# Moving the split weight tiles and the gated products of the MLPs by 64 bytes in SBUF

## The chip, the core and the metric

The kernel runs on one core of a Trainium2 chip. The metric is the device time of one execution in microseconds (us); smaller is better.

## The reference

A trunk of two layers over 512 tokens with 1024 channels, all in float32. Layer 0 is an mLSTM mixer, layer 1 a causal convolution module, and each is followed by the same kind of gated MLP. Ahead of every part stands an RMSNorm, behind it a residual sum.

```python
def conv_ffn(x, w_up, conv_w, conv_b, w_down):          # w_up 1024 x 5632, w_down 2816 x 1024
    hdn = causal_dwconv(x @ w_up, conv_w, conv_b)       # 3 taps
    return (jax.nn.silu(hdn[..., :D_FF]) * hdn[..., D_FF:]) @ w_down

for i in range(2):
    h = rmsnorm(x, norm_mix[i])
    x = x + (mlstm_mixer(h, ...) if i == 0 else conformer_conv_mixer(h, ...))
    x = x + conv_ffn(rmsnorm(x, norm_ffn[i]), f_w_up[i], f_conv_w[i], f_conv_b[i], f_w_down[i])
return rmsnorm(x, norm_final)
```

## The kernel before

Channels lie on the 128 partitions and the 512 tokens along the free axis. Each product of two float32 values is made of three float32r products: both sides are split into a high part (rounded to float32r) and a low part (the rest), and `mm3` (L160 to L163) issues high x high (L161), high weights x low input (L162) and low weights x high input (L163). Every matmul has its own weight load, which the engine can run beside the matmul ahead of it.

Weights come as units of 128 x 1024 floats in the order of their use. `feed_to` (L135) starts their transfers on the SP queue into `wr` (L140, four buffers), copies the high part on ScalarE (L149, tile `wh`) and subtracts on VectorE (L150, tile `wl`); `wh` and `wl` have three buffers each. `next_unit` (L154) hands a unit out with two more split ahead.

The stages in order of time, with what stands still in the array (the stationary side) and what streams through it (the moving side, named first in the profile's rows):

- `v_pair`: here the weights stream, and slices of the normed input `xh`, `xl` are stationary: 192 matmuls of 512 columns.
- `proj` (L404) for queries, keys and output gates, and, in layer 1, for the input of the convolution module (`glu`): weights stationary, `xh`, `xl` moving: 384 matmuls in each layer.
- attention: small products between tiles of the pool `mlstm`.
- `out_proj` (L560): weights stationary, the gated heads `gh`, `gl_` (layer 0) or the normed convolution `zht`, `zlt` (layer 1) moving: 192 matmuls each (L161 to L163, L576, L577, L580).
- `ffn` (L593), once per layer. Up: 22 pairs of `proj`, so 22 x 2 x 8 x 3 = 1056 matmuls with `xh`, `xl` moving. VectorE and ScalarE make the gated product from them and split it into `yh`, `yl` (L616, L617). Down: 8 output blocks of 22 x 3 = 66 matmuls with `yh`, `yl` moving: 528 in layer 0; in layer 1 the last block is done in two halves of 256 columns, which leaves 462 of 512 columns.

Where a tile lies follows from the pools, which are laid down one behind the other in the order in which they are opened: `const` (L49, with `xh`, `xl`), `wraw` (`wr`), `wsp` (`wh`, `wl`), `work` (sums and scratch tiles), and behind it whichever of `mlstm`, `ffn`, `conv` is open. Byte offsets within a partition, worked out from the sizes:

| tiles | offset of the first | modulo 128 | step from one to the next |
|---|---|---|---|
| `xh`, `xl` | 38464 | 64 | 2048 |
| `wr` | 71232 | 64 | 4096 |
| `wh`, `wl` | 87616 | 64 | 4096; a unit's k-th block of 128 columns lies 512 further each |
| `work` | 112192 | 64 (scratch tiles), 32 (`rsb`) | 2048 |
| `yh`, `yl` of both MLPs | 124672, 169728 | 0 | 2048 |
| `zht`, `zlt` | 175744, 194176 | 0 | 2048 |
| `gh`, `gl_` of heads 0 to 3 | 141568, 158080 | 0, 32, 64, 96 | 4128 |

The scores `sh` of the attention, the queries and keys `qkh`, `qkl`, and the selectors `sel` lie at 0 modulo 128, the constants `onesr`, `invdr` of the norms at 32.

Of the kernel before, what the change touches and what calls it, by code (L numbers as in the profile page):

```python
# [14 lines left out]
P = 128  # L15
# [9 lines left out]
EPS = 1e-6  # L25
QSCALE = 128.0 ** -0.5
NEG = -1.0e30
NPH = 4                    # token phases of the convolution on the tensor engine
NTAU = T // NPH
NJ = (CK + 2 * NPH - 3) // NPH  # L30
GR = 68                    # rows: input gates at 0, running maximum at 32, forget gates at 64

# column offsets in the packed per-channel parameter array
_COLS = {}
_off = 0
for _n, _w in [("norm_mix", 16), ("norm_ffn", 16), ("norm_final", 8), ("mconv_w", 32),
# [9 lines left out]
def hybrid_trunk(ctx, tc, x_in, par_in, tph_in, wg_in, wv_in, wqk_in, wo_in, mout_in, cin_in,  # L46
# [5 lines left out]
    wraw = ctx.enter_context(tc.tile_pool(name="wraw", bufs=4))  # L52
    wsp = ctx.enter_context(tc.tile_pool(name="wsp", bufs=3))
    work = ctx.enter_context(tc.tile_pool(name="work", bufs=1))
    psum = ctx.enter_context(tc.tile_pool(name="psum", bufs=6, space=bass.MemoryType.PSUM))
    psms = ctx.enter_context(tc.tile_pool(name="psms", bufs=2, space=bass.MemoryType.PSUM))

# [9 lines left out]
    def small():  # L67
        return psms.tile([P, T], F32, tag="ms", name=nm("ms"))

# [1 line left out]
    par = const.tile([P, NPAR], F32, name="par")  # L71
    nc.scalar.dma_start(out=par[:, :16], in_=par_in[:, :16])

# [18 lines left out]
    G.memset(mhalf, -0.5)  # L92

    def warm(n, after=None):
        """Products that nobody reads, to keep the clock of the tensor engine up over a wait."""
        ps = bank()
        for _ in range(n):
            with tc.issue_after(after.ins) if after is not None else nullcontext():
                after = PE.matmul(ps[:, :P], ones, ones, start=True, stop=True)  # L99

# [1 line left out]
    seq = []  # L102
    for h in range(2):
        for u in range(4):
# [57 lines left out]
        PE.matmul(ps, lh, rl, start=False, stop=False)  # L162
        PE.matmul(ps, ll, rh, start=False, stop=stop)  # L163

# [1 line left out]
    xh = [None] * KD  # L166
    xl = [None] * KD

# [27 lines left out]
        return t[:, c].rearrange("p (a b) -> p a b", b=P)  # L196

    def to_rows(src, c, tag):
        """Values along the free axis, equal on all partitions -> [128 tokens, blocks]."""
        nb = (c.stop - c.start) // P  # L200
        dg = work.tile([P, T], F32, tag="tmp", name=nm("dg"), bufs=4)
        V.tensor_tensor(out=blocks(dg, c), in0=src,
                        in1=ident[:].unsqueeze(1).to_broadcast([P, nb, P]), op=ALU.mult)
        r4 = work.tile([P, NTB], F32, tag=tag, name=nm(tag))
        V.tensor_reduce(out=r4[:, :nb], in_=blocks(dg, c), op=ALU.add, axis=mybir.AxisListType.X)
        return r4

    def from_rows(r4, nb, pb):
        """[128 tokens, blocks] -> the values along the free axis on all partitions (PSUM)."""
        hl = work.tile([P, 2, NTB], F32R, tag="hl", name=nm("hl"))  # L210
        V.tensor_copy(hl[:, 0, :nb], r4[:, :nb])
        V.tensor_tensor(out=hl[:, 1, :nb], in0=r4[:, :nb], in1=hl[:, 0, :nb], op=ALU.subtract)
        for i in range(2):
            dg = work.tile([P, NTB, P], F32R, tag="tmp", name=nm("dgr"), bufs=4)
            v = V.tensor_tensor(out=dg[:, :nb], in0=ident[:].unsqueeze(1).to_broadcast([P, nb, P]),
                            in1=hl[:, i, :nb].bitcast(F32).unsqueeze(2).to_broadcast([P, nb, P]),
                            op=ALU.mult)
            p = PE.matmul(pb, onesr, dg[:, :nb].rearrange("p a b -> p (a b)"), start=i == 0, stop=i == 1)  # L218
        return v, p

    def col_mean(ps, t, c, w):
        """Sum over the partitions of t times the constant in w, on all partitions."""
        h = work.tile([P, T], F32R, tag="tmp", name=nm("ch"), bufs=4)
        l = work.tile([P, T], F32R, tag="tmp", name=nm("cl"), bufs=4)
        A.copy(h[:, c], t[:, c])
        V.tensor_tensor(out=l[:, c], in0=t[:, c], in1=h[:, c], op=ALU.subtract)
        PE.matmul(ps, w, h[:, c], start=True, stop=False)
        PE.matmul(ps, w, l[:, c], start=False, stop=True)
# [4 lines left out]
        return o4  # L233

    def row_sums(ps, t, c, w, start, stop):
        """Adds the sums over the partitions of t, times w, to ps: [128 tokens, 2 * blocks]."""
        nb = (c.stop - c.start) // P
        for b in range(nb):
            s = slice(c.start + b * P, c.start + (b + 1) * P)
            PE.matmul(ps[:, 2 * b : 2 * b + 2], t[:, s], w[:, :2], start=start and b == 0,  # L240
                      stop=stop and b == nb - 1)

    def norm_rows(nrm, c):
        """1 / rms of the tokens in c, [128 tokens, blocks]."""
        n = c.stop - c.start
        ps = small()
        col_mean(ps[:, :n], nrm.acc, c, invdr)
        r4 = to_rows(ps[:, :n].rearrange("p (a b) -> p a b", b=P), c, "ms4")
        V.tensor_scalar(out=r4[:, : n // P], in0=r4[:, : n // P], scalar1=EPS, scalar2=None,
                        op0=ALU.add)  # L250
        return rsqrt4(r4, n // P, "rs4")

    # the row factors of a norm are worked out between the first products of the next stage
    hooks = []

    def run_hook():
# [15 lines left out]

    rs = {}

    # ================= layer 0: mLSTM =================
    warm(9)
    nrm = Norm()
    first = wraw.tile([P, 1024], F32, tag="wr", name="wr0")
# [76 lines left out]

    pv = v_pair(0)

    # gates, channel-major: input gates on partitions 0-3, forget gates on 32-35
    wgh, wgl = next_unit()
    pg = small()  # L360
    for k in range(KD):
# [77 lines left out]
    T0 = [0, 128, 256, 256]  # L439

    def att_decay(h):
        """exp of the decay from s to t less the running maximum; s on partitions, t free."""
        plf, pm = small(), small()
        for p, i in ((plf, h), (pm, NH + h)):
            PE.matmul(p, sel[:, i, :], sth, start=True, stop=False)
            PE.matmul(p, sel[:, i, :], stl, start=False, stop=True)
        es = []
        for i in range(NTB):
            t0 = T0[i]
            w = T - t0  # L450
            o = P + t0 - i * P
            e = mp.tile([P, T], F32, tag="se", name=nm("se"), bufs=4)
            V.tensor_tensor_scan(e[:, :w], plf[:, t0:], fm[:, o : o + w], NEG, ALU.add, ALU.max)  # L453
            es.append((i, t0, w, e))
        for i, t0, w, e in es:
            V.scalar_tensor_tensor(out=e[:, :w], in0=e[:, :w], scalar=li4[:, i, h : h + 1],
                                   in1=pm[:, t0:], op0=ALU.add, op1=ALU.subtract)
            A.activation(e[:, :w], e[:, :w], AF.Exp)
        return es
# [68 lines left out]
    q = qk(0)  # L528
# [60 lines left out]
    out_proj(gh, gl_, None, lambda m: ("norm_ffn", m))  # L589
    mctx.close()  # L590

    # ================= gated MLP with a depthwise convolution =================
    def ffn(l, g=None, last=False):  # L593
        fctx = ExitStack()
        fp = fctx.enter_context(tc.tile_pool(name=nm("ffn"), bufs=1))
        yh = fp.tile([P, NF, T], F32R, name=nm("yh"))
        yl = fp.tile([P, NF, T], F32R, name=nm("yl"))
        for j in range(NF):
# [91 lines left out]

    ffn(0, lambda m: ("norm_mix", 8 + m))

    # ================= layer 1: convolution module =================
    cctx = ExitStack()
    cp = cctx.enter_context(tc.tile_pool(name="conv", bufs=1))
    DVE_CH, POOL_CH, PE_CH = (0, 2, 4), (1,), (3, 5, 6, 7)
# [4 lines left out]
    pdvr = cp.tile([P, P], F32R, name="pdvr")  # L701
    A.copy(pdvr, p128)
    cacc = {c: cp.tile([P, T], F32, name=f"cacc{c}") for c in range(8)}
    # 1 where the partition lies in the block of NPH partitions
    tph = cp.tile([P, 8 * 4 * NJ * NPH], F32, name="tph")
    nc.sync.dma_start(out=tph, in_=tph_in)
    msk4 = cp.tile([P, P // NPH, 1], F32, name="msk4")
# [74 lines left out]
                o = 32 * (2 * hf + g)  # L782
                (nc.scalar if g == 0 else nc.sync).dma_start(out=back[o : o + 32], in_=co[:, g])

    # taps for the vector engine and GpSimd, handed out between the products
    vtaps, gtaps = [], []

    def background(nv, ng):
# [9 lines left out]
    FIRST, LAST = PE_CH[0], PE_CH[-1]  # L798

    def shift():  # L800
        """The mean of one block of channels, by which all values are shifted before their sums."""
        d[FIRST] = cp.tile([P, T], F32, name=f"d{FIRST}")
        A.activation(d[FIRST].rearrange("p (t q) -> p t q", q=NPH),
                     cacc[FIRST].rearrange("p (q t) -> p t q", q=NPH), AF.Identity,
# [56 lines left out]
    sq4 = stats(4, V)  # L861
    sq7 = stats(LAST, None)

    # layer norm over channels
    pr1, pr2, pmu = small(), small(), bank()
    for i, (t1, t2) in enumerate(((s1, s2), (d[LAST], sq7))):
        row_sums(pr1, t1, slice(0, T), invd, i == 0, i == 1)
# [34 lines left out]
def _layout(inputs):  # L902
    f = {k: np.asarray(v) for k, v in inputs.items()}

    def ch(a):  # [..., C] -> [128, ... * C/128], channel c = m * 128 + p
        a = a.reshape(a.shape[:-1] + (-1, P))
        return np.moveaxis(a, -1, 0).reshape(P, -1)

    def taps(w):  # [K, C] -> [128, C/128 * K]
        k, c = w.shape  # L910
        return w.reshape(k, c // P, P).transpose(2, 1, 0).reshape(P, -1)

    def cols(w, n=P):  # [K, N] -> [N/n, 128, K/128 * n]
        k, c = w.shape
        return w.reshape(k // P, P, c // n, n).transpose(2, 1, 0, 3).reshape(c // n, P, -1)

    # gate biases: input gates on partitions 0-3, forget gates on 32-35
    bg = np.zeros((P, 1), np.float32)
    bg[0:4, 0], bg[32:36, 0] = f["m_b_gates"][0][:4], f["m_b_gates"][0][4:]
    # taps by token phase: dph[c * NPH + p, m, g, j, q] = w[K - 1 - (NPH * j + q - p), m * 128 + g * 32 + c]  # L920
    dw = f["c_dw_w"][0].reshape(CK, KD, 4, P // 4)
    dph = np.zeros((P // NPH, NPH, KD, 4, NJ, NPH), np.float32)
    for p in range(NPH):
# [50 lines left out]
```

## Time and profile before

| | |
|---|---|
| median of 2 runs | 1194.37 us (1194.08 to 1194.66) |
| profiled execution, first to last instruction (span) | 1191.0 us |
| TensorE matmul busy | 1134.3 us (95%) |
| TensorE weight load busy | 939.7 us (79%) |
| VectorE busy | 788.6 us (66%) |
| ScalarE busy | 510.8 us (43%) |
| GpSimd busy | 174.8 us (15%) |

The page gives the span of the profiled execution and not its whole time; the median of the runs lies 3.4 us above that span. Matmuls overlap in the records: one begins before the end of the one ahead of it. So two numbers are read below: the distance from start to start of matmuls in a row (what a matmul costs), and the recorded length of one (the "mean ns"), which is some 162 ns longer than the distance and moves with it.

### The profile page before, as it was taken

Reading aid. Unit: us, or ns where it says so; the run is one execution under the profiler, and the core shown is the slowest. Engines: PE = TensorE matmul, PEld = TensorE weight load, DVE = VectorE, ACT = ScalarE, POOL = GpSimd, SP = SyncE. Lnnn points to the kernel's source line nnn. Section 1 sums busy time; section 2 is a strip of 40 time slices with the busy share of each in tenths; the row PEclk is TensorE's granted clock in tenths of the full one; section 3 lists DMA queues with packets and bytes.
Section 4 is the critical chain, followed back from the end, with each engine's and each line's share of the span. In section 5 each row is a group of like instructions: output and inputs, shape, how many; then the busy total and the mean of one; then the engine's idle time right before and its main releaser. Section 6 shows DMA issues by size and latency. Waiting matters only on the chain.

```text
span 1191.0 us, 13476 instructions
## 1 busy us (share of the span) xinstructions
PE 1134.3 (95%) x5226; PEld 939.7 (79%) x5226; DVE 788.6 (66%) x1022; ACT 510.8 (43%) x713; POOL 174.8 (15%) x126
## 2 busy tenths in 40 slices
PE   9999999999999999999998757699999999999996
PEld 7788888888888888888887647588888888888886
DVE  6788875487777775332479999874877777752222
ACT  6556774354444443222244522363544444432221
POOL 4000001100000000000267857021000000000002
PEclk9999999999999999999998879699999999999998
DMA  6222123223232323233332112022232323233322
GB/s 247 89 89 71 54 74 103 90 89 106 89 106 89 105 86 92 90 97 98 110 105 62 62 44 67 14 88 89 92 103 90 106 89 106 84 98 89 93 62 71
DMA packets 36369, 106.85 MB, mean 90 GB/s; under 512 B 4049, under 2 KB 10321, under 8 KB 36305
## 3 DMA queue, kind: packets, MB, share of 16 engines
q1 hardware_dynamic: 31728, 103.25, 27.2%
q10 hardware_dynamic: 4576, 2.74, 0.8%
q8 instruction: 41, 0.67, 0.2%
q14 instruction: 24, 0.19, 0.0%
HBM read 101.78 MB, written 2.10 MB: 87 GB/s over the span
## 4 chain that ended last, share of the span: by engine, by line
PE 84%; DVE 13%; issue 1%; ACT 1%; DMA 1%; POOL 0%; ACTq 0%; POOLq 0%; SPq 0%; DVEq 0%
PE mm L161 25%; PE mm L162 25%; PE mm L163 25%; DVE cacc L744 8%; PE mm L580 2%; PE mm L577 2%; PE mm L576 2%; DVE wl L150 2%; PE ms L240 1%; PE mm L99 0%; DMA xall<-in_dram 0%; PE ms L218 0%; DVE u L722 0%; DVE se L453 0%; DVE s L826 0%
## 5 line engine op out<-in xcount | busy, mean ns | idle before, releaser
L163 PE MATMUL mm<-xh,wl 128*128 128x512 f32 x960 | 375.6, 391 | 3.3 <-DVE wl L150 3.3
L161 PE MATMUL mm<-xh,wh 128*128 128x512 f32 x960 | 375.6, 392 | 0.0
L162 PE MATMUL mm<-xl,wh 128*128 128x512 f32 x960 | 375.4, 391 | 0.0
L150 DVE TENSOR_TENSOR wl<-wr,wh 128x1024 fp32r<-128x1024 f32 (+1 forms) x192 | 236.5, 1235 | 165.5 <-ACT wh L149 163.3
L149 ACT CAST wh<-wr 128x1024 fp32r<-128x1024 f32 (+1 forms) x192 | 197.4, 1030 | 296.1 <-PE mm L162 243.6
L163 PEld LDWEIGHTS mm<-xh,wl 128*128 128x128 f32 x960 | 181.4, 189 | 41.9 <-DVE wl L150 3.7
L162 PEld LDWEIGHTS mm<-xl,wh 128*128 128x128 f32 x960 | 181.4, 189 | 37.9
L161 PEld LDWEIGHTS mm<-xh,wh 128*128 128x128 f32 x960 | 181.5, 189 | 37.2
L193 POOL TENSOR_TENSOR acc<-acc,sq 128x512 f32<-128x512 f32 x30 | 43.3, 1444 | 746.7 <-ACT sq L191 746.2
L161 PE MATMUL mm<-yh,wh 128*128 128x512 f32 (+1 forms) x374 | 142.3, 380 | 0.0
L162 PE MATMUL mm<-yl,wh 128*128 128x512 f32 (+1 forms) x374 | 142.3, 380 | 0.0
L163 PE MATMUL mm<-yh,wl 128*128 128x512 f32 (+1 forms) x374 | 142.2, 380 | 0.0
L606 DVE TENSOR_TENSOR mm<-mm,rsb 128x512 f32<-128x512 f32 x88 | 60.8, 695 | 76.0 <-PE mm L163 73.1
L744 DVE SCALAR_TENSOR_TENSOR cacc<-u,par,cacc 128x501 f32<-128x501 f32 (+27 forms) x80 | 102.1, 1321 | 0.1
L161 PEld LDWEIGHTS mm<-yh,wh 128*128 128x128 f32 x374 | 70.0, 187 | 15.5
L162 PEld LDWEIGHTS mm<-yl,wh 128*128 128x128 f32 x374 | 70.0, 187 | 15.3
L163 PEld LDWEIGHTS mm<-yh,wl 128*128 128x128 f32 x374 | 70.0, 187 | 15.2
L616 ACT CAST yh<-ta 128x512 fp32r<-128x512 f32 x44 | 27.3, 620 | 104.6 <-DVE ta L615 104.6
L611 DVE SCALAR_TENSOR_TENSOR ta<-mm,par,ta 128x511 f32<-128x511 f32 x88 | 65.6, 745 | 1.3
L611 DVE SCALAR_TENSOR_TENSOR tb<-mm,par,tb 128x511 f32<-128x511 f32 x88 | 65.5, 746 | 1.4
L614 ACT ACTIVATE ta<-ta 128x512 f32<-128x512 f32 x44 | 27.8, 632 | 79.4 <-DVE ta L611 79.4
L741 POOL TENSOR_TENSOR cacc<-cacc,cprod 128x511 f32<-128x511 f32 (+29 forms) x30 | 49.5, 1651 | 24.1 <-ACT cprod L739 22.4
(237 smaller groups left out, 1200.5 us busy)
## 6 DMA issues: line engine op xcount, KB each, us to landing
wr<-in_dram SPq DMA_DIRECT2D x175, 512.0 KB, 3.5
wr<-in_dram SPq DMA_DIRECT2D x16, 384.0 KB, 3.1
xall<-in_dram SPq DMA_DIRECT2D x8, 256.0 KB, 6.4
us<-u ACTq DMA_DIRECT2D x16, 64.0 KB, 2.1
out_dram<-xall SPq DMA_DIRECT2D x2, 384.0 KB, 3.5
tph<-in_dram SPq DMA_DIRECT2D x1, 576.0 KB, 4.5
wr<-in_dram SPq DMA_DIRECT2D x2, 256.0 KB, 3.9
cacc<-co ACTq DMA_DIRECT2D x8, 64.0 KB, 2.4
```

The costliest lines, as they stand in the source:

```text
L149: st["last"] = A.copy(hi[:, :n], r[:, :n])
L150: V.tensor_tensor(out=lo[:, :n], in0=r[:, :n], in1=hi[:, :n], op=ALU.subtract)
L161: PE.matmul(ps, lh, rh, start=start, stop=False)
L162: PE.matmul(ps, lh, rl, start=False, stop=False)
L163: PE.matmul(ps, ll, rh, start=False, stop=stop)
L193: e.tensor_tensor(out=nrm.acc[:, c], in0=nrm.acc[:, c], in1=sq[:, c], op=ALU.add)
L606: V.tensor_tensor(out=ps, in0=ps, in1=rs["b"], op=ALU.mult)
L611: V.scalar_tensor_tensor(out=t[:, s:], in0=ps[:, : T - s], scalar=pcol("fconv_w", m * 3 + 2 - s), in1=t[:, s:], op0=ALU.mult, op1=ALU.add)
L614: A.activation(ta, ta, AF.Silu)
L616: A.copy(yh[:, j, :], ta)
L741: G.tensor_tensor(out=a[:, s:], in0=a[:, s:], in1=p[:, s:], op=ALU.add)
L744: V.scalar_tensor_tensor(out=cacc[j][:, s:], in0=u[:, : T - s], scalar=dw(j, CK - 1 - s), in1=cacc[j][:, s:], op0=ALU.mult, op1=ALU.add)
```

## The change

One tile of 64 bytes per partition that nothing uses is put at the head of the pool `wsp`, and one more at the head of the pool of the first MLP. No instruction is added or taken away. The rest of the diff takes out comments and docstrings, so the lines of the later code move up by a few.

```diff
     wsp = ctx.enter_context(tc.tile_pool(name="wsp", bufs=3))
     work = ctx.enter_context(tc.tile_pool(name="work", bufs=1))
+    wsp.tile([P, 16], F32, tag="pad", name="pad", bufs=1)
     psum = ctx.enter_context(tc.tile_pool(name="psum", bufs=6, space=bass.MemoryType.PSUM))
...
     def ffn(l, g=None, last=False):
         fctx = ExitStack()
         fp = fctx.enter_context(tc.tile_pool(name=nm("ffn"), bufs=1))
+        if l == 0:
+            fp.tile([P, 16], F32, name=nm("pad"))
         yh = fp.tile([P, NF, T], F32R, name=nm("yh"))
```

What moves, modulo 128: `wh`, `wl` from 64 to 0; everything behind them by 64 too, so `work` from 64 to 0, `zht`, `zlt` from 0 to 64, `gh`, `gl_` from 0, 32, 64, 96 to 64, 96, 0, 32, and `sh`, `qkh`, `qkl`, `sel` from 0 to 64; `yh`, `yl` of the second MLP from 0 to 64; those of the first MLP by 128, so they stay at 0. `xh`, `xl`, `wr` and the constants stay where they are.

## Rows read from the trace of the kernel before

**Rows 1.** The page, parts 1 and 4: span, busy times, chain by engine.

```profile
span 1191.0 us, 13476 instructions
PE 1134.3 (95%) x5226; PEld 939.7 (79%) x5226; DVE 788.6 (66%) x1022; ACT 510.8 (43%) x713; POOL 174.8 (15%) x126
...
PE 84%; DVE 13%; issue 1%; ACT 1%; DMA 1%; POOL 0%; ACTq 0%; POOLq 0%; SPq 0%; DVEq 0%
```

**Rows 2.** Busy time by stretch; columns as in the first line.

```profile
core 0: us, PE busy (x) PEld busy (x) DVE busy (x) ACT busy (x) POOL busy (x), PEclk, DMA share, GB/s
57.00:183.00 126.00, 125.07 (x637) 105.91 (x636) 103.09 (x193) 84.60 (x155) 4.04 (x4) 1.00 0.22 75
220.00:460.00 240.00, 240.00 (x1060) 198.67 (x1059) 175.63 (x226) 106.99 (x134) 1.02 (x1) 1.00 0.30 96
460.00:584.00 124.00, 124.00 (x534) 99.38 (x533) 39.90 (x43) 33.66 (x41) 7.77 (x6) 1.00 0.31 93
620.00:757.00 137.00, 93.33 (x521) 80.76 (x519) 136.90 (x122) 50.26 (x77) 92.62 (x54) 0.85 0.19 58
785.00:815.00 30.00, 30.00 (x133) 24.62 (x132) 19.64 (x21) 16.65 (x22) 9.25 (x6) 1.00 0.37 123
```

**Rows 3.** Groups by form, whole span: busy us, mean ns of one.

```profile
L161 PE MATMUL mm<-xh,wh 128*128 128x512 f32 x960 | 375.6, 392 | 0.0
L161 PE MATMUL mm<-yh,wh 128*128 128x512 f32 x330 | 130.0, 394 | 0.0
L162 PE MATMUL mm<-wl,xh 128*128 128x512 f32 x64 | 23.5, 389 | 0.0
```

**Rows 4.** Groups by form in 230 to 455 us, up of the first MLP.

```profile
L161 PE MATMUL mm<-xh,wh 128*128 128x512 f32 x330 | 128.4, 389 | 0.0
```

**Rows 5.** Groups by form in 462 to 582 us, down of the first MLP.

```profile
L161 PE MATMUL mm<-yh,wh 128*128 128x512 f32 x172 | 67.8, 394 | 0.0
```

**Rows 6.** Groups by form, output products of layer 1, then of layer 0.

```profile
L577 PE MATMUL mm<-zlt,wh 128*128 128x512 f32 x41 | 16.1, 392 | 0.0
...
L577 PE MATMUL mm<-gl,wh 128*128 128x512 f32 x46 | 18.1, 395 | 0.0
```

**Rows 7.** Timeline in the first up: start, length, instruction; two of 28.

```profile
399.78 0.39 PE L162 MATMUL mm<-xl,wh 128*128 128x512 f32 x1
...
405.90 0.39 PE L162 MATMUL mm<-xl,wh 128*128 128x512 f32 x1
```

**Rows 8.** Timeline in the first down: first and last of 27.

```profile
519.79 0.39 PE L162 MATMUL mm<-yl,wh 128*128 128x512 f32 x1
...
525.86 0.39 PE L161 MATMUL mm<-yh,wh 128*128 128x512 f32 x1
```

**Rows 9.** Timeline in the output product of layer 1: two, 13 steps apart.

```profile
787.84 0.39 PE L576 MATMUL mm<-zht,wh 128*128 128x512 f32 x1
...
790.81 0.39 PE L577 MATMUL mm<-zlt,wh 128*128 128x512 f32 x1
```

**Rows 10.** Groups by form in 93.70 to 93.72 us: the last matmul before attention.

```profile
L163 PE MATMUL mm<-xh,wl 128*128 128x512 f32 x1 | 0.4, 388 | 0.0
```

**Rows 11.** Groups by form in 592.56 to 592.59 us: the matmul before a norm's.

```profile
L162 PE MATMUL mm<-xl,wh 128*128 128x512 f32 x1 | 0.4, 396 | 0.0
```

**Rows 12.** Groups by form in 460.97 to 460.98 us: the first of down.

```profile
L161 PE MATMUL mm<-yh,wh 128*128 128x512 f32 x1 | 0.4, 394 | 0.0
```

**Rows 13.** Groups by form in 131.90 to 132.70 us: selectors, both sides at 0.

```profile
L445 PE MATMUL ms<-sth,sel 68*128 68x512 f32 x2 | 0.8, 396 | 0.0
```

**Rows 14.** Groups by form, VectorE, whole span: tiles at 0, then at 64.

```profile
L617 DVE TENSOR_TENSOR yl<-ta,yh 128x512 fp32r<-128x512 f32 x44 | 30.4, 691 | 26.1 <-ACT yh L616 26.1
...
L226 DVE TENSOR_TENSOR cl<-acc,ch 128x512 fp32r<-128x512 f32 x4 | 2.8, 689 | 2.1 <-ACT ch L225 2.1
```

**Rows 15.** Groups, GpSimd, whole span: sums at 0, then at 64.

```profile
L741 POOL TENSOR_TENSOR cacc<-cacc,cprod 128x511 f32<-128x511 f32 (+29 forms) x30 | 49.5, 1651 | 24.1 <-ACT cprod L739 22.4
L193 POOL TENSOR_TENSOR acc<-acc,sq 128x512 f32<-128x512 f32 x30 | 43.3, 1444 | 746.7 <-ACT sq L191 746.2
```

## The prediction

> **What bounds the kernel now.** The page comes first. TensorE is busy for 1134.3 of 1191.0 us and holds 84% of the chain that ended last; VectorE has 13% of it [rows 1]. The stretches then say where each of the two rules. In 220 to 460 us (up of the first MLP), 460 to 584 (its down) and 785 to 815 (output product of layer 1) TensorE is busy for the whole stretch, at a granted clock of 1.00, which is the level of 2.4 GHz. Only in 620 to 757 us, the convolution, is VectorE the full one (136.90 of 137.00 us), and TensorE has 93.33 us to do there [rows 2]. So almost everywhere the time is the number of matmuls times the distance from one to the next, and nothing else has to be late.
>
> Then that distance, stage by stage, because every stage streams the same 512 columns. At 2.4 GHz they would take 213.3 ns. In up, 27 steps take 405.90 - 399.78 = 6.12 us: 226.7 ns each [rows 7]. In down, 26 steps take 6.07 us, so about 233.4; the records come as 233, 233 and 234, and I use 233.3 [rows 8]. In the output product of layer 1, 13 steps take 2.97 us: 228.5 [rows 9]. The recorded length of one follows the distance and is read to the ns: 389, 394 and 392 [rows 4 to 6]; layer 0's output product has 395 [rows 6]. The number of matmuls, their clock and their weight loads are alike, so something else costs 6.6 ns per matmul in down. What differs is where the operands lie: up has the moving input at 64 and the weights at 64 modulo 128, down has the moving product at 0 and the weights at 64. The change moves just these.
>
> **The change part by part.** The two pads issue nothing: no instruction, no transfer, no wait, and no queue gets another order. Their cost can only come through addresses.
>
> *Copies, sums and transfers.* VectorE takes 691 ns for 512 elements with its tiles at 0 and 689 with them at 64 [rows 14]: I take 0. GpSimd's sums take 1651 ns at 0 and 1444 at 64 [rows 15], but the first run in the convolution beside a full VectorE and the second mostly do not, so the place need not be the cause. Were it, 30 taps would gain 0.2 us each, 6 us of GpSimd's time, and VectorE's bound would hide some of it: 0 to -6 us, taken as 0. Transfers land in `wr`, which stays.
>
> *Up: 2 x 1056 matmuls, weights from 64 to 0, input still at 64.* No long run of this pair exists before. Its nearest row is a matmul of `xh` beside which a weight block at 0 is loaded: it took 388 ns [rows 10], against 389 in the run of up [rows 4]. That is the last product of a `proj` before attention; there are eight such places (blocks of `sh`, `qkh` and `sel`), and all eight have 388. Where the next weights lie at 32 instead (the constants of a norm, twelve places with the same length), the same matmul takes 396 [rows 11], so one matmul does show a bad place at once; and the first matmul of down shows 394 [rows 12], the length of all that follow [rows 5]. Hence I take 0 for up. The bounds are -1 ns each (-2.1 us) and, if single cases mislead, the step of down, +6.6 ns each.
>
> Here the Trainium skill speaks against any effect (SBUF — State Buffer, section "Who interferes with whom"): the array reads its moving operand and its weights through two ports of their own. The two spacings of this trace, for equal work, do not agree with ports alone; by that rule the sum would be 0.
>
> *Second down: 462 matmuls, weights at 0, product from 0 to 64.* This is the pair of up after the change. If up keeps 226.7, down gets it too: 462 x 6.6 = -3.1 us. The bounds are that and 0.
>
> *First down: 528 matmuls, weights at 0, product at 0.* The nearest row has both at 0: the four selector products, 396 and 394 in mean [rows 13]. So 394 stays, and I take 0; the bounds are -3.5 us (528 x 6.6, if equal places are what counts) and +0.5 us (1 ns more).
>
> *Products of layer 0.* In `v_pair` the weights stream, so the moving side goes to 0 over stationary slices at 64, the pair of down before: 192 matmuls at 389 [rows 3] go to 394, +1.3 us. `proj` for queries, keys and gates is as up: 384 x 0. In attention and in the output product of layer 0 both sides move by 64 together: 0, with 192 x 6.6 = 1.3 us either way as the bound.
>
> *Layer 1.* The 384 matmuls of `glu` are as up, and where VectorE is full they lie beside it anyway. The output product's moving side goes from 0 to 64: 192 x (228.5 - 226.7) = -0.3 us.
>
> The sum: -3.1 - 0.3 + 1.3 = -2.1 us on a span of 1191.0, so 1188.9. The median of the runs lies 3.4 us above the span, so 1192.3.
>
> **The rivals.**
>
> *A, the sum above: the moving side's own place decides.* For it: rows 10 and 12. Against it: `zlt`, at 0 like `yh`, has 392 and not 394 [rows 5, 6], so modulo 128 is not the whole rule. About 1192; its own range is 1187 to 1195.
>
> *B, slower: what counts is whether the two sides lie alike.* Up is alike before (64 and 64) and fast, down is not (0 and 64) and slow. After the change up is unlike, by as much as down was. Then 2112 x 6.6 = +14.0 us, `proj` of layer 0 384 x 6.6 = +2.5, `v_pair` +1.3, `glu` some +1 (only its units ahead of 620 us), the first down becomes alike, -3.5, and the second stays unlike. Together +15.3: 1210. For it: the long runs are the bulk of the evidence and fit it. Against it: the eight matmuls of 388 with unlike sides, and selectors that are alike and slow [rows 10, 13]. It decides over A once up's distance grows by 2.1 / 2112 = 1.0 ns, to 227.7.
>
> *C, the place does nothing here.* The difference between up and down would come from something that they don't share, such as the second stream of VectorE and ScalarE beside up. All distances stay: 1194.4. The Trainium skill's rule of two ports, above, would have this one. Against it: twelve matmuls in the midst of a `proj`, with the same work around them, are 7 ns longer where the next weights lie at 32 [rows 11].
>
> *D, between A and B: up drifts.* The 388 of rows 10 is a little under up's steady 389, so a run of such matmuls may not hold its beat and, like the output product of layer 1, pay on some and not on others: 228.5 ns, 1.8 more. Then 2112 x 1.8 = +3.8, `proj` and `glu` +1, `v_pair` +1.3, second down 462 x (233.3 - 228.5) = -2.2: +3.9, 1198.
>
> *E, the floor falls.* No matmul of 512 columns is read below 388 in these rows, so 226.7 looks like the floor of this kernel. If weights at 0 took one more step of 6.6 ns away, up and `proj` would give 14.0 + 2.5 + 1 and the second down 3.1 and more: about 1173. The Trainium skill has 512 columns following each other by 512/2.4 + 2.5 ns, an estimate of 215.8 (TensorE: Matmul & The Clock Gate, section "Back-to-back issue gap"). No run of this trace comes near that.
>
> **How the numbers follow.** A 0.42, B 0.20, D 0.20, C 0.12, E 0.04, others 0.02. The time of the likeliest is 1192. A, C and D lie in 1187 to 1199 and hold 0.74, so the range must take in B, up to 1211; below 1187 lies E, which I leave out: 1187 to 1211. Faster or slower by over 2%, about what a measurement of this kernel can tell from no change, is under 1170.5 or over 1218.3. E reaches the first only with every bound at its end (0.02). B passes the second only if up's matmuls go to 396, or past it, and not to 394: 2112 x 8.3 = 17.5, with `proj`, `v_pair` and `glu` some 1217 to 1219 (0.03). All else, 0.95, is within 2%.
>
> **What would show it.** In the groups of the changed kernel: `xh` by `wh` in up at 388 or 389 (A, C, E lower) or at 394 (B) or between (D); `yh` by `wh` at 394 in the first MLP and 389 in the second (A), or 389 in the first and 394 in the second (B). `v_pair` at 394 speaks for A and B alike. The convolution's stretch should keep its 137 us of VectorE; if it shrinks, the GpSimd row was about the place after all. The prediction is wrong if up's length leaves 388 to 389: that one row carries 2112 matmuls, and each ns on it is 2.1 us.

## The result: 14 us longer, and the loss is in the up projections

The changed kernel takes 1208.17 us (2 runs, 1207.98 to 1208.37) against 1194.37 us before: the ratio is 1.012, 95% interval 1.0091 to 1.0149. That is less than 2%, but it is slower, where a gain of 2 us was forecast, and inside the range of 1187 to 1211, which reached that far because it took in rival B's 1210. The order of instructions on every engine is the one of before.

The page of the changed kernel answers to [rows 1]: span, busy time of each engine, shares of the chain that ended last.

```profile
span 1206.3 us, 13476 instructions
PE 1149.2 (95%) x5226; PEld 940.6 (78%) x5226; DVE 791.3 (66%) x1022; ACT 508.2 (42%) x713; POOL 174.6 (14%) x126
...
PE 84%; DVE 13%; issue 2%; ACT 1%; DMA 1%; POOL 0%; ACTq 0%; POOLq 0%; SPq 0%; DVEq 0%
```

The span grew by 15.3 us and TensorE's busy time by 14.9; every other engine moved by less than 3 us. That is 1.5 us more than the growth of the time, and the 3.4 us between span and time of the kernel before are no constant: in every other execution whose span is known the time lies 1.7 us above it, and a later execution of the kernel before with the same span of 1191.0 took 1192.74 us. So the profiled execution of the kernel before was a shorter one than the two that gave its time. The changed kernel's profiled execution has some 1.4 us at the start of layer 0 that this one lacks and that are no part of the change (last section); without them the span grew by 13.9. Where that lies is told by the groups by form (busy us, mean recorded length in ns). Of the changed kernel, in order: up of the first MLP (230 to 455 us), up of the second (850 to 1080), down of the first (480 to 590), down of the second (1100 to 1200), `v_pair` (12 to 50), output product of layer 1 (808 to 828), and of layer 0 (196 to 222). The lines of `mm3` are L162 to L164 here.

```profile
L162 PE MATMUL mm<-xh,wh 128*128 128x512 f32 x321 | 126.9, 395 | 0.0
...
L162 PE MATMUL mm<-xh,wh 128*128 128x512 f32 x316 | 125.0, 396 | 0.0
...
L162 PE MATMUL mm<-yh,wh 128*128 128x512 f32 x162 | 63.0, 389 | 0.0
...
L162 PE MATMUL mm<-yh,wh 128*128 128x512 f32 x113 | 44.7, 396 | 0.0
...
L163 PE MATMUL mm<-wl,xh 128*128 128x512 f32 x47 | 16.9, 391 | 0.0
...
L578 PE MATMUL mm<-zlt,wh 128*128 128x512 f32 x23 | 9.0, 391 | 0.0
...
L578 PE MATMUL mm<-gl,wh 128*128 128x512 f32 x39 | 15.4, 395 | 0.0
```

Up went from 389 [rows 4] to 395, the first down from 394 [rows 5] to 389; both output products stayed [rows 6]. The timeline in up (start, length, instruction) answers to [rows 7]:

```profile
398.67 0.40 PE L164 MATMUL mm<-xh,wl 128*128 128x512 f32 x1
398.90 0.39 PE L162 MATMUL mm<-xh,wh 128*128 128x512 f32 x1
399.13 0.40 PE L163 MATMUL mm<-xl,wh 128*128 128x512 f32 x1
...
401.00 0.40 PE L162 MATMUL mm<-xh,wh 128*128 128x512 f32 x1
```

Ten steps take 401.00 - 398.67 = 2.33 us: 233 ns from start to start, against 226.7 before. To the ns the steps alternate between 236 and 231, mean 233.3. The settled mean step is called the beat below. The recorded length is a rougher sign of it than [rows 4 to 6] suggested: a beat of 233.3 goes with 394 in down before, with 395 and 396 here, and with 397 and 398 in two runs below. Every time "from start to start" below is worked out in this way, over all the matmuls of its kind.

The stages, each from its first matmul to the first of the next, and the last one to the end of the span, in us (the output product of layer 0 took 45.1 in all of these and has no column; worked out from the same start times; the two kernels with half of the change and some others from below stand beside it):

| kernel | layer 0 to its output product | up 0 | down 0 | glu and convolution | output product 1 | up 1 | down 1 | span |
|---|---|---|---|---|---|---|---|---|
| before | 169.01 | 240.34 | 123.20 | 187.14 | 44.21 | 240.33 | 135.34 | 1191.0 |
| changed | 172.69 | 247.31 | 119.70 | 187.80 | 44.42 | 247.31 | 135.34 | 1206.3 |
| e_onlyw | 171.26 | 247.31 | 123.20 | 187.73 | 45.20 | 247.30 | 135.15 | 1208.6 |
| e_onlyp | 169.01 | 240.34 | 119.68 | 186.87 | 44.41 | 240.37 | 135.35 | 1187.5 |
| e_wsp256 | 170.57 | 240.34 | 123.20 | 186.83 | 44.43 | 240.34 | 135.34 | 1192.7 |
| e_y64 | 171.00 | 240.34 | 119.68 | 186.87 | 44.42 | 240.35 | 133.00 | 1187.2 |
| e_best | 169.02 | 240.34 | 119.68 | 186.63 | 44.09 | 240.32 | 132.82 | 1184.5 |

Both ups lose 7.0 us, the first down gains 3.5, the second stays: rival B, term by term.

### The profile page after: what moved, and what is told of

It is laid out like the page before. It is cut to its first block, busy times and chain, and to the rows that moved or that the text cites. A ratio compares the mean times of both kernels' runs of the same rounds, so it can differ in the third digit from the quotient of the medians.

```text
span 1206.3 us, 13476 instructions
## 1 busy us (share of the span) xinstructions
PE 1149.2 (95%) x5226; PEld 940.6 (78%) x5226; DVE 791.3 (66%) x1022; ACT 508.2 (42%) x713; POOL 174.6 (14%) x126
## 4 chain that ended last, share of the span: by engine, by line
PE 84%; DVE 13%; issue 2%; ACT 1%; DMA 1%; POOL 0%; ACTq 0%; POOLq 0%; SPq 0%; DVEq 0%
PE mm L162 25%; PE mm L163 25%; PE mm L164 25%; DVE cacc L747 8%; PE mm L581 2%; PE mm L578 2%; PE mm L577 2%; DVE wl L151 2%; PE ms L241 1%; DMA xall<-in_dram 0%; PE ms L219 0%; DVE u L725 0%; DVE se L454 0%; DVE s L829 0%; PE mm L518 0%
## 5 line engine op out<-in xcount | busy, mean ns | idle before, releaser
L164 PE MATMUL mm<-xh,wl 128*128 128x512 f32 x960 | 380.7, 397 | 3.5 <-DVE wl L151 3.5
L162 PE MATMUL mm<-xh,wh 128*128 128x512 f32 x960 | 381.0, 397 | 0.0
L163 PE MATMUL mm<-xl,wh 128*128 128x512 f32 x960 | 380.8, 397 | 0.0
L164 PEld LDWEIGHTS mm<-xh,wl 128*128 128x128 f32 x960 | 181.2, 189 | 47.8 <-DVE wl L151 3.9
L162 PEld LDWEIGHTS mm<-xh,wh 128*128 128x128 f32 x960 | 181.2, 189 | 43.2
L194 POOL TENSOR_TENSOR acc<-acc,sq 128x512 f32<-128x512 f32 x30 | 43.5, 1451 | 757.0 <-ACT sq L192 756.5
L162 PE MATMUL mm<-yh,wh 128*128 128x512 f32 (+1 forms) x374 | 141.7, 379 | 0.0
L164 PE MATMUL mm<-yh,wl 128*128 128x512 f32 (+1 forms) x374 | 141.6, 378 | 0.0
L162 PEld LDWEIGHTS mm<-yh,wh 128*128 128x128 f32 x374 | 70.3, 188 | 14.0
L163 PEld LDWEIGHTS mm<-yl,wh 128*128 128x128 f32 x374 | 70.3, 188 | 13.9
L164 PEld LDWEIGHTS mm<-yh,wl 128*128 128x128 f32 x374 | 70.3, 188 | 13.8
L744 POOL TENSOR_TENSOR cacc<-cacc,cprod 128x511 f32<-128x511 f32 (+29 forms) x30 | 49.1, 1635 | 25.4 <-ACT cprod L742 23.7
```

The costliest lines, as they stand in the source:

```text
L162: PE.matmul(ps, lh, rh, start=start, stop=False)
L194: e.tensor_tensor(out=nrm.acc[:, c], in0=nrm.acc[:, c], in1=sq[:, c], op=ALU.add)
L744: G.tensor_tensor(out=a[:, s:], in0=a[:, s:], in1=p[:, s:], op=ALU.add)
```

## The experiments

Four readings were open. **Distance** (rival B in a sharper form): what counts is how far the moving operand lies from the weights, modulo some length. **Own place**: the place of one side alone decides (the forecast, A). **Modulo 128**: as the distance, but 64 and 192 are the same thing, and 128 is no distance. **No place at all** (C). Offsets from here on are in bytes modulo 256, and a distance is the moving operand's offset less the stationary one's. By it, before: up 0 (64 and 64), down 192 (0 and 64), output product of layer 1 64 (128 and 64). After: up 192 (64 and 128), first down 0 (128 and 128), second down 192 (64 and 128), output product of layer 1 64 (192 and 128).

### Everything moved together (e_all64), and the gated products alone (e_y64)

`e_all64` puts a pad ahead of `xh` and all that follows it in memory:

```diff
+    const.tile([P, 16], F32, name="pad")
     mhalf = const.tile([P, 4], F32, name="mhalf")
```

`e_y64` puts one ahead of the gated products, in both MLPs:

```diff
+        fp.tile([P, 16], F32, tag="pad", name=nm("pad"), bufs=1)
         yh = fp.tile([P, NF, T], F32R, name=nm("yh"))
```

> The kernel before with everything from the normed input on moved by 64, so that both sides of every product move together: input and weights at 0, products of the MLPs at 64 modulo 128. Theories R and P: every distance stays, so 1194.4 us, up at 389 ns of length and down at 394. Rival M, by which weights at 0 are what made the changed kernel slow: up at 396 and some 1208 us.

> The kernel before with the gated products of both MLPs moved from 0 to 64 modulo 128 and the weights left at 64. Theory R: the distance of product and weights becomes 256, so both downs go from 233.3 to 226.7 ns: 990 x 6.6 = 6.5 us less, 1187.8 us, ratio 0.9945. Rival P: the same. Rival C (the place counts for nothing in down): 1194.4.

`e_all64` has the weights at 128, as the changed kernel has them, and the normed input moved along to 128. It took 1193.5 us, ratio 1.0008 [0.9998, 1.0018]. Its groups in up and in the first down, by form:

```profile
L162 PE MATMUL mm<-xh,wh 128*128 128x512 f32 x331 | 128.8, 389 | 0.0
...
L162 PE MATMUL mm<-yh,wh 128*128 128x512 f32 x165 | 65.0, 394 | 0.0
```

So the loss of the change is gone although the weights keep the address that they have in the changed kernel: their own place costs nothing. `e_y64` leaves the weights at 64 and puts the gated products there too (distance 0). It took 1187.8 us, ratio 0.9954 [0.9939, 0.9969]. That it met the forecast to the tenth is luck: the forecast started from 1194.4 us, and against 1192.8 for the kernel before in the same session the gain is 5.0 us and not 6.5. Down fell from 394 to 389 in both MLPs:

```profile
L161 PE MATMUL mm<-yh,wh 128*128 128x512 f32 x162 | 63.0, 389 | 0.0
```

The stages show 3.5 us of gain in the first down, as due for 528 x 6.6, but 2.3 in the second, where 462 x 6.6 = 3.0 were due. The rest went back in its last block, whose 132 products have 256 columns. The groups by form there, of before (1163 to 1190 us) and of `e_best` (1155 to 1183 us; below, the same places as `e_y64` in the MLPs):

```profile
L162 PE MATMUL mm<-yl,wh 128*128 128x256 f32 x44 | 12.3, 279 | 0.0
...
L162 PE MATMUL mm<-yl,wh 128*128 128x256 f32 x44 | 12.5, 285 | 0.0
```

From start to start these have a median of 113 to 114 ns before (distance 192) and of 120 in both later kernels (distance 0): at this width distance 0 is the slower one, and 132 products lose 0.8 us.

### The two halves of the change (e_onlyw, e_onlyp)

`e_onlyw` has the weight pad alone:

```diff
+    wsp.tile([P, 16], F32, tag="pad", name="pad", bufs=1)
```

`e_onlyp` has the MLP pad alone:

```diff
+        if l == 0:
+            fp.tile([P, 16], F32, name=nm("pad"))
```

> The weight half of the change alone: 64 bytes ahead of the split weight tiles, so that the weights lie at 128 modulo 256, and the gated products, which follow in memory, at 64 in both MLPs (in the changed kernel they were at 128 in the first). Distance theory (a beat is set by the moving operand's place less the weights', modulo 256; 0 gives 226.7 ns, 192 gives 233.3): up projections 233.3 as in the changed kernel, and both down projections at distance 192, so the first down projection loses what it had gained there: 384 products by 6.6 ns = 2.5 us above the changed kernel, so about 1210.7 us. Rival, the weights' own place alone sets the beat: the down projection of the first MLP stays at 226.7 ns as in the changed kernel, 1208.2 us.

> The other half alone: 64 bytes ahead of the gated products of the first MLP, nothing else. Weights at 64, gated products of the first MLP at 64, of the second at 0 as before. Distance theory: only the first down projection changes, 233.3 to 226.7 ns, 384 products by 6.6 = 2.5 us less than the kernel before, ratio 0.998. Rival, the weights' own place alone sets the beat: ratio 1.000, the first down projection stays at 233.3. Together with the other half the two should add up to the whole change: about +16.3 and -2.5 us.

`e_onlyw` took 1210.07 us, ratio 1.014 [1.0123, 1.0156]; `e_onlyp` 1189.04, ratio 0.9962 [0.9947, 0.9977]. The 2.5 us in both expectations was worked out with 384 products; the first down has 528, so 3.5 us were due, which is what the stages show (123.20 and 119.68). The two add up: +17.1 and -3.9 us against +13.8 for the whole change. The first down is slow again where only the weights moved (485 to 590 us, against 389 in the changed kernel), so the weights' own place is refuted here as well:

```profile
L162 PE MATMUL mm<-yh,wh 128*128 128x512 f32 x151 | 59.7, 396 | 0.0
```

One row of `e_onlyw` had not been expected, its output product of layer 1 (808 to 828 us):

```profile
L578 PE MATMUL mm<-zlt,wh 128*128 128x512 f32 x24 | 9.5, 398 | 0.0
```

Its operands lie at the very bytes where the changed kernel has them, and yet it runs at 398 and 233.3 ns from start to start, where the changed kernel has 391 and 228.9. At distance 64 the addresses alone don't fix the beat.

### The low weights 64 bytes off the high ones (e_wl64)

```diff
+    wsp.tile([P, 16], F32, tag="pad", name="pad", bufs=1)
     lo = wsp.tile([P, 1024], F32R, tag="wl", name="wl0")
```

> The kernel before with 64 bytes between the high and the low parts of the weights: wh at 64, wl at 0, and the products of the MLPs at 64. In up and down the distance is 0 for wh and 192 for wl. Theory R with the weights that are loaded beside a product: the product ahead of each one with wl (xl by wh) is long, the other two are not, some 228.9 ns on average, 1194.4 + 2112 x 2.2 - 990 x 4.4 = 1194.7 us. If the weights that stand in the array count, the product with wl is the long one, with the same average. If one long product shifts the phase for the others, all three forms change.

Here `wh` lies at 64 and `wl` at 128, so in up only one product in three, the one with `wl`, is off distance 0; it is at 192. It took 1205.1 us, ratio 1.0098 [1.0083, 1.0113]. In up, by form:

```profile
L163 PE MATMUL mm<-xh,wl 128*128 128x512 f32 x324 | 128.8, 397 | 0.0
L162 PE MATMUL mm<-xl,wh 128*128 128x512 f32 x324 | 127.0, 392 | 0.0
L161 PE MATMUL mm<-xh,wh 128*128 128x512 f32 x324 | 126.1, 389 | 0.0
```

From start to start these are 235.8, 229.2 and 228.4 ns: the product that uses the odd block is the long one, and the two behind it, which are at distance 0, don't come back to 226.7 before the next odd one. The mean, 231.1, is 4.4 above the floor, though two products of three are at distance 0: one odd block in three spoils the beat of all. The expectation had two of its readings come true together (the weights in the array count, and one long product shifts the others); its mean of 228.9 ns and its 1194.7 us were missed.

### The distance by itself (e_probe, e_probe2)

```diff
+            for b in list(range(0, 512, 16)) + [4, 8]:
+                run([b], [0])
+            for b in range(64, 512, 64):
+                run([0], [b])
+            run([0], [0, 0, 64, 64], 24)
+            run([0], [0, 0, 0, 0, 64, 64, 64, 64], 24)
```

> The kernel before with 786 more products ahead of the second MLP's down, which nobody reads; they cost what they take, so its time is not compared. 512 columns of yh move over blocks of yl; the distance of the moving side from the weights (modulo 512) is raised in steps of 16 bytes by moving the first (18 products each), then in steps of 64 by moving the second, then two mixed orders. Theory R (only the distance of the two sides modulo 256 counts): 226.7 ns from start to start at distance 0 and 256, 228.9 at 64 and 320, 233.3 at 192 and 448, and the same figures whichever side is moved; at 128 and 384 some value between 226 and 234. Rival P (only like or unlike modulo 128 counts): 226.7 at 0, 128, 256, 384 and one and the same slow value at 64, 192, 320, 448. Rival M (a side's own place counts): moving the weights by 64 does not give what moving the products by 448 gives. In the mixed orders a weight block at another distance should lengthen the product beside which it is loaded, or the one after it.

> Extra products, which nobody reads, ahead of the second down projection: runs of 18 at one distance, each of the first thirteen behind 18 products at distance 0, with the weights at 0, 64, 128 and 192. Question: in the first probe distance 64 took 233.3 ns behind a run at distance 48 and 228.9 ns behind a run at 0 (there the weights, not the moving operand, were shifted). If the history decides: distance 64 behind a run at 0 takes 228.9 ns whatever the weights' place, and 233.3 where a run at 32, 48 or 192 stands ahead of it. If the place decides: 233.3 with the moving operand at 64 and the weights at 0, 228.9 with the weights at 192, whatever stands ahead. Distance 192: 233.3 with every place if the distance alone decides. Steps of 4 bytes up to 256: the floor of 226.7 ns is a single place or a plateau from 240 on. With 384, 256 and 128 columns in place of 512: if the loss sits in the change from one product to the next it stays about 6.6 ns for a product of any length; if it goes with the words read, it shrinks to 3.3 ns at 256 columns.

The cut is from `e_probe`: a run is 18 products of `yh` blocks over `yl` blocks, with the moving side moved by `b` bytes in the first loop and the stationary side in the second. The products stand ahead of the second down and nobody reads them; each of the two kernels was executed once. From start to start, settled, 512 columns, ns (the steps of a run cycle through up to seven lengths, so the means are good to some 0.3):

```
distance      0    16    32    48    64    80    96   112   128   144   160   176   192   208   224   240   256
e_probe    226.7 231.5 233.5 233.3 233.3 231.0 233.1 231.0 232.5 233.3 234.0 233.4 233.3 234.6 233.3 226.7 226.7
e_probe2   226.7 231.8 233.2 230.0 228.9 231.5    -     -  233.2    -     -     -  233.3    -     -  236.7 226.7
```

From 272 to 496 `e_probe` repeats the values of 16 to 240 within 0.2 ns: the period is 256. Moving the stationary side instead gave 228.9 at distance 64, 233.3 at 192 and 226.7 at 256. A row by form for each of two settled runs: distance 0 in `e_probe2` (1253 to 1256 us, entered at 256) and 64 in `e_probe` (1073.3 to 1076.2 us):

```profile
L627 PE MATMUL mm<-yh,yl 128*128 128x512 f32 x15 | 3.6, 389 | 0.0
...
L627 PE MATMUL mm<-yh,yl 128*128 128x512 f32 x14 | 3.4, 397 | 0.0
```

"Modulo 128" and "no place" fall: 64, 128 and 192 all cost. In `e_probe2` distances 64 and 192 were run with the stationary side at 0, 64, 128 and 192, and 128 with it at 0, 64 and 128: the means did not differ by over 1 ns with the place. But 64, 48 and 240 have two beats each. Distance 64 came as 228.5 to 229.2 all eleven times in `e_probe2`, behind runs at 0, 32, 48, 80, 128 and 192, and as 233.3 behind 48 in `e_probe`. So neither theory in that expectation holds: the run before, as I had it, does not decide, and the place does not. Distance 240, at the same offsets, was 226.7 in `e_probe` (388) and 236.7 in `e_probe2`, here at 1119.3 to 1122.3 us and at 1236.5 to 1239.3 us:

```profile
L627 PE MATMUL mm<-yh,yl 128*128 128x512 f32 x15 | 3.6, 388 | 0.0
...
L627 PE MATMUL mm<-yh,yl 128*128 128x512 f32 x14 | 3.5, 400 | 0.0
```

Between 240 and 256 there is no plateau: 238.6 at 244, 233.3 at 248, 230.0 at 252. Only distance 0 was at 226.7 every time that it had settled. What picks one of two beats stays open. The run ahead and the place together are not ruled out: distance 64 with the moving side at 64 and the weights at 0 did not stand behind 48 again in `e_probe2`, and 240 stood behind 224 in `e_probe` and behind 232 in `e_probe2`.

The mixed runs show how a beat is entered and left. With four blocks at distance 0 and four whose weights lie 64 further (distance 192), in turns, the steps were (ns, from the start times; a bar where the blocks change):

```
228 233 230 226 | 236 231 236 229 | 231 231 235 232 | 226 236 231 235 | 229 232 231 226 | 236 231 235
```

In the first and the third turn the last product at distance 0 keeps its 226, though the load beside it is already that of the odd block, and the product that uses this block takes 236; in the second turn, entered before the beat had settled, the 236 comes one product later. The way back is slow: four products at distance 0 take 231, 231, 235, 232 in one turn and 229, 232, 231, 226 in the other. Runs of 18 at distance 0 settled at once or after up to ten steps (in `e_probe2` once 230, 236, 228, 233, 231, then 226.7).

Shorter products do not follow the same table (`e_probe2`, settled, one run each below 512, ns):

```
columns   distance 0     64    128    192
512            226.7  229.0  233.2  233.3
384            173.3  173.3  176.0  174.6
256            120.0  117.7  118.7  113.3
128            111.8  111.6  112.0  111.5
```

The loss is neither a fixed sum for each product nor in proportion to its words: at 256 columns distance 192 is the fastest and 0 the slowest, 6.7 ns apart, as in the last block of the second down, and at 128 no difference over 0.5 ns is left. The rows by form at 256 columns, for distance 0 (1270 to 1271 us) and 192 (1276 to 1277.3 us):

```profile
L627 PE MATMUL mm<-yh,yl 128*128 128x256 f32 x11 | 1.5, 283 | 0.0
...
L627 PE MATMUL mm<-yh,yl 128*128 128x256 f32 x14 | 1.8, 277 | 0.0
```

### The period in the whole kernel (e_wsp128, e_wsp256)

The pad of `e_wsp128`; in `e_wsp256` it has 64 columns in place of 32:

```diff
+    wsp.tile([P, 32], F32, tag="pad", name="pad", bufs=1)
```

> 128 bytes ahead of the split weight tiles: weights at 192 modulo 256, norm outputs left at 64, so the up projections are at distance 128; gated products at 128 (distance 192, as before), the conv module's output at 0 (distance 64, as before). Distance theory with period 256 and the probe's 232 to 232.5 ns at 128: 2112 up products by 5.3 to 5.8 ns = 11 to 12 us more, and some 2 us from the projections of layer 0: 1206 to 1208 us. Rival, only the place modulo 128 counts: 1194 us, up stays at 226.7 ns. The output products of layer 1 move their operand at 0 here and at 128 before, both 64 above the weights: the same 228.9 ns if the distance alone decides, 233.3 if the moving operand's own place takes part (the probe had 233.3 at distance 64 with the moving operand at 64).

> 256 bytes ahead of the split weight tiles: every distance is the same modulo 256 as in the kernel before, every one but that of products with all operands behind the pad is off by 256 modulo 512. Distance theory with period 256: no change, ratio 1.000, up projections 226.7 ns, down projections 233.3 ns. Rival, period 512 or more (the probe went only to 496 bytes with one pair of tiles): up projections 233 ns, some +14 us.

`e_wsp128` took 1212.27 us, ratio 1.0153 [1.0138, 1.0168]; `e_wsp256` 1192.69, ratio 1.0 [0.999, 1.0009]. Up in the one and in the other:

```profile
L162 PE MATMUL mm<-xh,wh 128*128 128x512 f32 x321 | 126.8, 395 | 0.0
...
L162 PE MATMUL mm<-xh,wh 128*128 128x512 f32 x330 | 128.4, 389 | 0.0
```

A step of 128 is as bad as one of 64, a step of 256 costs nothing: the period is 256 and not 128. `e_wsp128` came out 4 to 6 us above its 1206 to 1208. Up at distance 128 takes 233.3 ns in mean here and not 232 to 232.5 (247.26 us for a stage, close to the changed kernel's), which is some 2 us of that. Layer 0 to its output product took 173.64 us, 4.6 more than before where some 2 were expected; 2.0 of these 4.6 are the long first products of the last section. And its second down, at distance 192 as before, shows that the distance does not fix the beat at 256 columns either: the last block has a median step of 118 ns where the kernel before has 113, and is 0.5 us longer. Its output product of layer 1 (moving at 0, weights at 192) kept 229 ns.

### All products of 512 columns of the two MLPs and of layer 1's output at distance 0 (e_best)

```diff
+        fp.tile([P, 16], F32, tag="pad", name=nm("pad"), bufs=1)
         yh = fp.tile([P, NF, T], F32R, name=nm("yh"))
...
+    cp.tile([P, 48], F32, name="pad")
     cacc2 = cp.tile([P, T], F32, name="caccp")
```

> The gated products of both MLPs and the conv module's output put at 64 modulo 256, where the weights lie: 64 bytes ahead of the gated products, 192 bytes at the head of the conv module's pool. Distance theory: up and down projections 226.7 ns, output products of layer 1 from 228.9 to 226.7 (192 by 2.2 ns = 0.4 us below the kernel that aligned the gated products alone): ratio 0.9952 against 0.9955 there. Rival, the gain of that kernel was not the distance of the gated products: output products stay at 228.9 and the ratio is that of the other kernel.

1186.68 us, ratio 0.9951 [0.9937, 0.9964]: below both kernels. The output product of layer 1 has the floor now (785 to 808 us), 226.7 ns from start to start:

```profile
L577 PE MATMUL mm<-zlt,wh 128*128 128x512 f32 x36 | 14.0, 389 | 0.0
```

Its stage is 0.32 us shorter than in `e_y64`, where 0.4 was forecast. Against `e_y64` as a whole the two intervals overlap, so that step alone is not shown by the times.

## Why the prediction was wrong

**What held.** TensorE bounds the kernel and the time is the count of matmuls times their distance from start to start: the changed kernel's 15.3 us are TensorE's 14.9 us of busy time and little else. That the operands' places set the beat of up held too (up is alike in everything but address in `e_all64` and the changed kernel); elsewhere the places alone do not fix it (228.9 or 233.3 at distance 64). Copies and sums at nothing held: GpSimd's two kinds of sums have changed places and kept their lengths (1635 and 1451 ns, against 1651 and 1444 [rows 15]), so their difference is not the place, and VectorE still fills 137.43 of the 140 us of the convolution's stretch (630 to 770 us).

**The step that failed: "Hence I take 0 for up."** It was read from the eight matmuls of 388 ns beside which a weight block at 0 is loaded [rows 10], backed by one that showed 396 at another place [rows 11]. Up went to 395 and lost 2 x 7.0 us; with it the second down, which was to gain 3.1 as the pair of up, gained nothing. The mixed run shows why [rows 10] misled: on the way from distance 0 to 192 the product *beside* the first odd load keeps its 226 ns, and the product that *uses* that block pays. The 388 belonged to a product whose own weights were still at distance 0; behind it came products of attention, with another moving tile. Nor were all such places at 388. Three more matmuls of `xh` in the trace of before stand ahead of a block at 0 modulo 128 and are long, at 57.37, 58.14 and 174.68 us (400, 397 and 398 ns; ahead of `st`, of a selector, as three of the eight, and of `hn`); the first and the last of them:

```profile
L163 PE MATMUL mm<-xh,wl 128*128 128x512 f32 x1 | 0.4, 400 | 0.0
...
L163 PE MATMUL mm<-xh,wl 128*128 128x512 f32 x1 | 0.4, 398 | 0.0
```

[rows 11] taught the wrong lesson (one matmul shows a bad place at once), since a single transition can go either way: in `e_probe2` the last product of a run at distance 0, with its moving side at 0, took 232 to 233 beside the load of a block at 128, and 226 to 227 beside blocks at 0, 64 and 192. The first matmul of down with its 394 [rows 12] was read as support for A; it fits B as well.

**The other terms.** With the distance rule in A's place the working of B gives the stages: up +14.0 (measured 6.97 + 6.98), first down -3.5 (measured -3.50), second down 0 (0.00). `v_pair` was put at +1.3 by both; it went to 391 and from 226.7 to 228.9 ns, 192 x 2.2 = +0.4, as its distance is 64 and not 192. `glu` had some +1 and shows 0.66. Layer 0 as a whole shows +3.7 where B had 2.5 + 1.3; some 1.4 us of that are no part of the change (last section). The output product of layer 1 was taken to gain 0.3 as its moving side came to 64; its distance stayed 64 and so did its beat.

**The selectors.** That they have both sides at 0 and are slow [rows 13] was held against B. They come four at a time behind products of other shapes, and the mixed run shows that four products at distance 0 need not be enough to come back to its beat. They should have weighed nothing.

**The other rivals.** A falls with `e_all64`: own places moved, and nothing changed. C falls with `e_y64` and `e_onlyp`. D had the right thought in one point, that a beat has values in between (228.9 at distance 64), but up got 233.3. E did not come: no settled run of 512 columns had a mean below 226.6. The rule of the Trainium skill (SBUF — State Buffer, section "Who interferes with whom") that the array's two reads go through ports of their own would leave no difference between distances; 226.7 against 233.3 ns in `e_all64` and the changed kernel, for equal work, does not agree with it.

**The weights of the evidence.** Two long runs of a thousand matmuls each pointed to B; eight single matmuls at a border pointed to A and got twice B's chance. That was the error in the chances.

## What to carry to other kernels

Where TensorE is busy throughout, read the mean distance from start to start of each stage to the tenth of a ns, and where equal products differ, compare the moving operand's offset less the stationary one's modulo 256: here distance 0 gave 226.7 ns for 512 float32r columns and nearly all others 229 to 239, so a pad of 64 bytes was worth 5 us or cost 14. Move both sides together or neither; measure again for other widths, since at 256 columns the order was turned round (113 ns at distance 192 in most kernels and 118 in `e_wsp128`, 120 at 0). Do not take a steady beat from a single matmul at a border between two patterns: the cost may fall on the next one, and a beat takes several products to settle.

## What the runs showed of the hardware that was not expected

- The beat depends on the distance modulo 256 in steps as small as 4 bytes (236.7 ns at 4, 233.4 at 8, 230.0 at 252), and is not smooth: 238.6 at 244, 226.7 at 256.
- One distance can have two steady beats with the same addresses: 228.9 and 233.3 at 64, 226.7 and 236.7 at 240. The cause is open.
- In some executions the first seven to ten products of `v_pair` follow each other by 427 ns in place of 227 to 233: in the changed kernel, `e_y64`, `e_wsp256`, `e_wl64`, `e_wsp128` and `e_probe2`, and not in before and the other five. That costs 1.4 us in the changed kernel and up to 2.1. The pads are not its cause, as `e_probe` and `e_probe2` have every tile of layer 0 at the same place and differ in it. It is why the layer 0 stage differs by up to 2 us between kernels with equal beats.

```profile
7.15 0.63 PE L163 MATMUL mm<-wl,xh 128*128 128x512 f32 x1
7.57 0.63 PE L162 MATMUL mm<-wh,xh 128*128 128x512 f32 x1
8.00 0.63 PE L163 MATMUL mm<-wl,xh 128*128 128x512 f32 x1
...
9.96 0.39 PE L164 MATMUL mm<-wh,xl 128*128 128x512 f32 x1
```

The granted clock of that stretch is given as 1.00, but that is no reading: the trace's records of the clock begin only at 9.74 us in the changed kernel and at 5.90 us in before, and a stretch without a record is given as 1.00. In all six executions with long products the records begin at 9.6 to 10.8 us, where the long products end, and in the other six at 4.2 to 5.9 us. And 427 ns is the step at the lower level of 1.2 GHz: in the convolution of before, at a granted clock of 0.50 (699 to 702 us), six steps take 701.95 - 699.39 = 2.56 us.

```profile
699.39 0.63 PE L162 MATMUL mm<-xl,wh 128*128 128x512 f32 x1
...
701.95 0.52 PE L162 MATMUL mm<-xl,wh 128*128 128x512 f32 x1
```

So these products most likely ran at the lower level. Why the clock rose later in some executions stays open: TensorE had done the same products ahead of them in all twelve.
